# 24 of 48 blocks of modulations move from the first layer's projections to its feed-forward part

## The chip, the core and the metric

The kernel runs on one core of a Trainium2 chip. The metric is the device time of one execution in microseconds (us), the median of several runs; lower is better. The engines are TensorE (PE in the profile; PEld is its weight load), VectorE (DVE), ScalarE (ACT), GpSimd (POOL) and SyncE (SP, whose queue issues nearly all loads here).

## The reference

A block of two layers is followed by two more ("hybrid") layers. Each of the four layers scales and shifts its input by modulations, which are a vector times a wide matrix, and which depend on nothing that the layers compute. Cut to what matters:

```
def adaln(cond, w, b):
    return jax.nn.silu(cond) @ w + b            # w: 1024 x 6144

def modulate(x, g, shift, scale):
    return rmsnorm(x, g) * (1 + scale) + shift

def even_layer(x, c, ctx, c_ctx, ...):          # the first layer
    sh_m, sc_m, gt_m, sh_f, sc_f, gt_f = jnp.split(adaln(c, mod_w, mod_b)[:, None, :], 6, axis=-1)
    sh_c, sc_c = jnp.split(adaln(c_ctx, mod_w, mod_b), 6, axis=-1)[:2]
    p = modulate(x, mix_pre_g, sh_m, sc_m) @ w_in
    uc = modulate(ctx, mix_pre_g, sh_c, sc_c)
    h_m = mlstm_mixer(...)                      # 8 heads
    h_d = diff_mixer(...)                       # 4 heads
    mix = jnp.concatenate([h_m, h_d], axis=-1) @ w_out
    x = x + gt_m * rmsnorm(mix, mix_post_g)
    y = swiglu(modulate(x, ffn_pre_g, sh_f, sc_f), ffn_w1, ffn_w3, ffn_w2)
    return x + gt_f * rmsnorm(y, ffn_post_g)

def odd_layer(...):                             # convolution, then 8 experts; modulations from its own mod_w
def hybrid_layer(x, c, w_ada, b_ada, ...):      # twice; shift, scale, gate from c @ w_ada + b_ada (1024 x 3072)
```

There are 256 tokens of width 1024, all in fp32.

## The kernel before

**The stream.** All weights pass through one list, `plan()` (L1933), which class `Stream` works off in order. An entry is two halves of up to 512 KB. `load_to` issues the two loads on SP's queue (L164) into a ring of RB = 8 buffers named `raw`; a load waits until the buffer eight loads back is free. Most entries are weight chunks: a half is split into a rounded part `hi` (ACT, L98) and the rest `lo` (DVE, L99; both are 128x1024), and then its `raw` buffer is free. The split parts lie in a ring of SB = 5 buffers until PE has used them, each product as three matmuls (L92 to L94). The order in the list is therefore the order of the loads.

**The modulations.** An entry can also be a block of a modulation: 128 rows of one third of a modulation matrix (class `Ada`; a third is a group of 8 blocks, and `it((l, i))` names group i of layer l). Its two halves are multiplied by that row's entry of the condition and added up in the tile `adac`: DVE does the first half (L339 for a group's first block, else L342), ACT scales the second half (L343; L340 for the first block) and POOL adds it in two pieces (L345). After the eighth block PE sums over the rows in 8 matmuls (L359) and transposes (L369), and DVE adds the bias (L372). The blocks of the hybrid layers' last groups, (2,1) and (3,1), have half the width, 512 KB for the whole block. Only group (0,0), which comes first, goes another way (L359 directly).

**The first layer.** `s[0]` is the input projection, 14 chunks in the order of `ORDER` (L486); `Mix0.project` takes one after another and puts the heads between them (table `AFTER`): `diff_unit` for a head of the differential attention, `mlstm_head` for the others. After the first chunk of keys the gates are made: a running maximum over time in 16 steps on DVE (L602), which ends in L612. Chunks with a rotary embedding go through `rope` on DVE (L668, L673, L675), which frees the PSUM bank for the next products. `s[1]` is the output projection, 4 chunks.

**The feed-forward part.** `swiglu_specs` gives 33 chunks: eleven steps of w1, w3 and the w2 of the step before, 1 MiB each. The products of w1 and w3 go to `ph`, those of w2 to `py`.

`weave(a, b, first)` (L1905) spreads list b evenly between the entries of a from entry `first` on. The tile framework then orders each engine's instructions by a timeline of its own when the program is built; on an engine they run in that order. The experts of the second layer get ten more `raw` buffers (RX).

Of the kernel before, what the change touches and what calls it, by code (L numbers as in the profile page):

```python
# [113 lines left out]
class Stream:  # L114
# [8 lines left out]
    def __init__(self, env, plan, ahead, split_ahead=1):  # L123
        self.env, self.plan = env, plan
        self.nd = self.ns = self.n = 0
        self.ahead, self.split_ahead = ahead, split_ahead
        self.raw, self.spl = {}, {}

        self.gain = {}

        self.every = self.turn2 = 0
        self.on_pool = set()
        self.pool, self.bufs, self.more, self.turn = env.rawp, env.raw_bufs, None, 0

        self.stop, self.hold = 1 << 30, (0, [])
# [85 lines left out]
def kchunk(w, n=256):  # L221

    return (4, n, [[(w[512 * n * h:512 * n * (h + 1)].rearrange("(p k f) -> p k f", p=128, k=4), 0, n)] for h in range(2)]), None
# [16 lines left out]
def rchunk(w, r0):  # L240

    return (1, 1024, [[(w[r0 + 128 * h:r0 + 128 * h + 128, :].rearrange("(a p) f -> p a f", p=128), 0, 1024)]
                      for h in range(2)]), None
# [252 lines left out]
def mix0_specs(w_in, w_out):  # L496
    return [kchunk(w_in[i]) for i in range(len(ORDER))], [rchunk(w_out, 256 * i) for i in (2, 3, 0, 1)]
# [445 lines left out]
def swiglu_specs(w1, w3, w2):  # L943
    s = []
    n = w1.shape[0]
    for i in range(n):
        s += [kchunk(w1[i]), kchunk(w3[i])]
        if i:
            s.append(rchunk(w2, 256 * (i - 1)))
    return s + [rchunk(w2, 256 * (n - 1))]  # L950
# [43 lines left out]
def conv_specs(pw1, pw2):  # L994
    s = []
    for i in range(4):
        s += [kchunk(pw1[4 * j + i]) for j in range(2)]
    return s + [rchunk(pw2, 256 * i) for i in range(4)]
# [129 lines left out]
def moe_specs(w1, w3, w2):  # L1128
    s = []
    for x in range(NE):  # L1130
        for i in range(STEPS):
            s += [kchunk(w1[x, i]), kchunk(w3[x, i])]
            if i:
                s.append(rchunk(w2[x], 256 * (i - 1)))
        s.append(rchunk(w2[x], 256 * (STEPS - 1)))
    return s
# [241 lines left out]
def hyb_specs(w_in, w_out, cmp_w1):  # L1378
    s, at = [], 0
    for c in CH:  # L1380
        n = sum(m for _, m in c)
        s.append(kchunk(w_in[D * at:D * (at + n)], n))
        at += n
    s.insert(8, ((1, 1024, [[(cmp_w1[i][:, None, :], 0, 1024)] for i in range(2)]), "raw"))
    return s + [rchunk(w_out, 256 * i) for i in OUT]
# [507 lines left out]

RB, SB, AH, SA, RX, MA, F1, NF = 8, 5, 5, 1, 10, 9, 2, 45


def load_tok(e, ap, t, q=None):
# [5 lines left out]
def weave(a, b, first=0):  # L1905

    out, j, n = list(a[:first]), 0, max(1, len(a) - first)
    for i, x in enumerate(a[first:]):
        k = len(b) * (i + 1) // n
        out += [x, *b[j:k]]  # L1910
        j = k
    return out + list(b[j:])


class Model:
# [17 lines left out]
    def plan(self):  # L1933
        self.moe_start = self.moe_end = 0
        I, it = self.I, self.items
        p = []
        if "l0_mod_w" in I:
            p += it((0, 0))
            s = mix0_specs(I["l0_w_in"], I["l0_w_out"])
            f = it((0, 1), (0, 2), (1, 0), (1, 1), (1, 2), (2, 0))  # L1940
            p += [s[0][0], ((1, D, [[(I["ctx"][0, 128 * b:128 * b + 128, :].rearrange("(a p) f -> p a f", p=128), 0, D)]
                                    for b in range(2)]), lambda *t: self.context(*t))]
            p += weave(s[0][1:], f[:NF], F1) + weave(s[1], f[NF:])
            self.ffn_start = len(p)
            p += weave(swiglu_specs(I["l0_ffn_w1"], I["l0_ffn_w3"], I["l0_ffn_w2"]), it((2, 1), (3, 0), (3, 1)))
        elif "l1_mod_w" in I:
            p += it((1, 0), (1, 1), (1, 2), (2, 0), (2, 1), (3, 0), (3, 1))
        else:
            p += it((2, 0), (2, 1), (3, 0), (3, 1))
        if "l1_mod_w" in I:  # L1950
            p += conv_specs(I["l1_conv_pw1_w"], I["l1_conv_pw2_w"])
            self.moe_start = len(p)
            p += moe_specs(I["l1_moe_w1"], I["l1_moe_w3"], I["l1_moe_w2"])
            self.moe_end = len(p)
        if "w_ada_2" in I:
            for l in range(2):
                p += hyb_specs(I["w_in_2"][l], I["w_out_2"][l], I["cmp_w1_2"][l])
        return p
# [372 lines left out]
```

## Time and profile before

| | |
|---|---|
| median of 3 runs | 1983.44 us (1973.08 to 2013.95) |
| the profiled execution | 1975.42 us, its span 1973.7 us |
| busy share of the span | PE 92%, PEld 82%, DVE 78%, ACT 60%, POOL 23% |
| SP's queue | 464.38 MB, 237 GB/s on the mean over the span |

The first layer's projections and heads run to about 345 us, the feed-forward part from 358 to 562 us, the convolution and the experts of the second layer to about 1540 us, the hybrid layers to the end. A window's row gives, after its stretch and length, busy time and count for PE, PEld, DVE, ACT and POOL, then the share of TensorE's clock that was granted (1.00 is 2.4 GHz, 0.50 is 1.2 GHz), the busy share of the DMA engines and GB/s. A row of the waits gives who waited for whom, the us in all, how often, and the longest. The timeline gives start and length in us.

### The profile page before, as it was taken

How to read it: one execution, taken by the hardware profiler on the slowest of the kernel's cores; microseconds unless marked ns; L12 is line 12 of the kernel's file. 1: busy time of each engine (PE TensorE's matmuls, PEld its weight loads, DVE VectorE, ACT ScalarE, POOL GpSimd, SP SyncE). 2: the span in 40 equal slices, each digit the busy share in tenths (PEclk: the TensorE clock that was granted, in tenths of full speed). 3: DMA queues.
4: the chain of work that ended last, by engine and by line, in shares of the span. 5: the costliest groups of instructions: out<-in, count | busy, mean ns of one | idle time of the engine just before them, and what ended most of it. 6: DMA issues, size and time to landing. Idle time of an engine off the chain costs nothing. (4 is left out here: it accounts for less than half of the span.)

```text
span 1973.7 us, 34412 instructions
## 1 busy us (share of the span) xinstructions
PE 1822.5 (92%) x13059; PEld 1616.2 (82%) x13059; DVE 1531.9 (78%) x2250; ACT 1179.1 (60%) x1804; POOL 454.0 (23%) x351
## 2 busy tenths in 40 slices
PE   6789989799979879999999999999999699989997
PEld 3678677699867568999999999999999589878886
DVE  5887898767664268999999999999998486659675
ACT  4455465655443346777777777777777454454443
POOL 1645664514211141000000000000000442533151
PEclk9889899899989989999999999999999799989999
DMA  9856666588763128999999999999996342344220
GB/s 360 280 182 214 213 227 238 179 269 302 244 247 119 39 80 296 367 348 333 351 363 347 337 351 363 350 330 353 364 352 241 110 142 74 100 128 132 76 76 22
DMA packets 132466, 468.49 MB, mean 237 GB/s; under 512 B 14994, under 2 KB 16274, under 8 KB 132292
## 3 DMA queue, kind: packets, MB, share of 16 engines
q1 hardware_dynamic: 131008, 464.38, 67.0%
q8 instruction: 105, 1.72, 0.4%
q10 hardware_dynamic: 1172, 1.66, 0.2%
q14 instruction: 69, 0.57, 0.1%
q0 software_dynamic: 112, 0.17, 0.1%
HBM read 465.10 MB, written 1.05 MB: 236 GB/s over the span
## 5 line engine op out<-in xcount | busy, mean ns | idle before, releaser
L99 DVE TENSOR_TENSOR lo<-raw,hi 128x1024 fp32r<-128x1024 f32 x694 | 871.7, 1271 | 170.8 <-ACT hi L98 146.1
L98 ACT CAST hi<-raw 128x1024 fp32r<-128x1024 f32 x734 | 762.9, 1048 | 280.4 <-PE ph L94 98.2
L94 PE MATMUL ph<-hi,gl 128*128 128x256 f32 x1408 | 397.7, 283 | 4.4 <-DVE gl L99 4.4
L93 PE MATMUL ph<-lo,gh 128*128 128x256 f32 x1408 | 397.0, 282 | 1.4 <-DVE lo L99 1.0
L92 PE MATMUL ph<-hi,gh 128*128 128x256 f32 x1408 | 394.6, 280 | 0.0
L93 PEld LDWEIGHTS ph<-lo,gh 128*128 128x128 f32 x1408 | 265.4, 188 | 9.9 <-DVE lo L99 5.8
L94 PEld LDWEIGHTS ph<-hi,gl 128*128 128x128 f32 x1408 | 265.4, 189 | 8.0 <-DVE gl L99 4.6
L92 PEld LDWEIGHTS ph<-hi,gh 128*128 128x128 f32 x1408 | 265.6, 189 | 2.8
L345 POOL TENSOR_TENSOR adac<-adac,raw 128x512 f32<-128x512 f32 x112 | 196.5, 1778 | 177.9 <-ACT raw L343 103.9
L1609 POOL MEMSET kv<- 64x2 f32 x4 | 0.4, 96 | 786.3 <-DVE lo L99 776.8
L93 PE MATMUL pe<-lo,hhi 128*128 128x512 f32 x352 | 137.8, 392 | 0.0
L92 PE MATMUL pe<-hi,hhi 128*128 128x512 f32 x352 | 136.9, 396 | 0.5 <-ACT hhi L98 0.5
L99 POOL TENSOR_TENSOR lo<-raw,hi 128x1024 fp32r<-128x1024 f32 (+1 forms) x40 | 97.0, 2433 | 146.1 <-ACT hi L98 120.0
L94 PE MATMUL pe<-hi,hlo 128*128 128x512 f32 x352 | 125.8, 392 | 0.0
L92 PE MATMUL ht<-hi,Hh 128*128 128x256 f32 (+1 forms) x384 | 115.2, 300 | 0.6 <-ACT u L461 0.6
L93 PE MATMUL ht<-lo,Hh 128*128 128x256 f32 (+1 forms) x384 | 114.3, 298 | 0.0
L94 PE MATMUL ht<-hi,Hl 128*128 128x256 f32 (+1 forms) x384 | 113.6, 296 | 0.0
L92 PE MATMUL ph<-Fh,hi 128*128 128x256 f32 x352 | 100.3, 287 | 8.0 <-DVE h L982 6.3
L93 PE MATMUL ph<-Fl,hi 128*128 128x256 f32 x352 | 100.0, 285 | 0.2 <-DVE Fl L475 0.2
L94 PE MATMUL ph<-Fh,lo 128*128 128x256 f32 x352 | 99.4, 285 | 0.0
L92 PEld LDWEIGHTS ht<-hi,Hh 128*128 128x128 f32 x384 | 77.5, 202 | 3.2 <-issue 1.4
L93 PEld LDWEIGHTS ht<-lo,Hh 128*128 128x128 f32 x384 | 77.2, 201 | 1.7 <-issue 1.5
(604 smaller groups left out, 3979.5 us busy)
## 6 DMA issues: line engine op xcount, KB each, us to landing
raw<-in_l_moe_w SPq DMA_DIRECT2D x528, 512.0 KB, 5.3
raw<-in_l_mod_w SPq DMA_DIRECT2D x96, 512.0 KB, 5.6
raw<-in_l_ffn_w SPq DMA_DIRECT2D x66, 512.0 KB, 4.6
raw<-in_w_in SPq DMA_DIRECT2D x60, 512.0 KB, 3.6
raw<-in_w_ada SPq DMA_DIRECT2D x32, 512.0 KB, 5.1
raw<-in_l_w_in SPq DMA_DIRECT2D x28, 512.0 KB, 6.1
raw<-in_l_conv_pw_w SPq DMA_DIRECT2D x24, 512.0 KB, 4.6
raw<-in_w_ada SPq DMA_DIRECT2D x32, 256.0 KB, 4.1
```

What stands on the lines that cost most here:

```text
L92: mm(out, a[0], b[0], start=start, stop=False, **kw)
L93: mm(out, a[0], b[1], start=False, stop=False, **kw)
L94: return mm(out, a[1], b[0], start=False, stop=stop, **kw)
L98: nc.scalar.copy(hi, src)
L99: (lo_eng or nc.vector).tensor_tensor(lo, src, f32(hi), op=OP.subtract)
L345: nc.gpsimd.tensor_tensor(a[:, 1, i:i + 512], a[:, 1, i:i + 512], y[:, i:i + 512], op=OP.add)
L1609: nc.gpsimd.memset(kv[64:128, :, T - 1:T], 0.0)
```

## The change

In the list, three groups of 8 blocks, (1,1), (1,2) and (2,0), move from the first layer to the feed-forward part, which now holds 48 blocks between its 33 chunks, in place of 24. The three groups left, (0,1), (0,2) and (1,0), are spread behind the projection's sixth chunk after the first one (F1 = 5, before 2), three blocks to a chunk; before it were four, and the last three of (2,0) stood between the chunks of the output projection. Nothing else is changed; the same bytes are loaded and the same sums made.

```
-RB, SB, AH, SA, RX, MA, F1, NF = 8, 5, 5, 1, 10, 9, 2, 45
+RB, SB, AH, SA, RX, MA, F1 = 8, 5, 5, 1, 10, 9, 5
...
-            f = it((0, 1), (0, 2), (1, 0), (1, 1), (1, 2), (2, 0))
+            f = it((0, 1), (0, 2), (1, 0))
...
-            p += weave(s[0][1:], f[:NF], F1) + weave(s[1], f[NF:])
+            p += weave(s[0][1:], f, F1) + s[1]
...
-            p += weave(swiglu_specs(I["l0_ffn_w1"], I["l0_ffn_w3"], I["l0_ffn_w2"]), it((2, 1), (3, 0), (3, 1)))
+            p += weave(swiglu_specs(I["l0_ffn_w1"], I["l0_ffn_w3"], I["l0_ffn_w2"]), it((1, 1), (1, 2), (2, 0), (2, 1), (3, 0), (3, 1)))
```

What stands on DVE ahead of the first `rope` (its first row is L668; `adac` is a modulation's sum, `lo` a weight chunk's rest, `u`, `Ul`, `qT` and `nlam` belong to the layer). Before:

```order
L342 SCALAR_TENSOR_TENSOR adac<-raw,cond_112,adac 128x1024
L99 TENSOR_TENSOR lo<-raw,hi 128x1024
L445 TENSOR_SCALAR u<-kT,g_464,modc 128x256 x2
L650 SCALAR_TENSOR_TENSOR qT<-cvt,cvy 128x256
L824 TENSOR_SCALAR nlam<-nlam 128x1
L446 TENSOR_TENSOR Ul<-u,Uh 128x2x256
L650 SCALAR_TENSOR_TENSOR qT<-cvt,cvy 128x256
L342 SCALAR_TENSOR_TENSOR adac<-raw,cond_112,adac 128x1024
L575 MEMSET lf 128x4x24
L99 TENSOR_TENSOR lo<-raw,hi 128x1024
L668 TENSOR_TENSOR rp_551<-pk,rope_291 128x256
L342 SCALAR_TENSOR_TENSOR adac<-raw,cond_112,adac 128x1024
```

The same place now:

```order
L824 TENSOR_SCALAR nlam<-nlam 128x1
L650 SCALAR_TENSOR_TENSOR qT<-cvt,cvy 128x256
L445 TENSOR_SCALAR u<-kT,g_464,modc 128x256
L99 TENSOR_TENSOR lo<-raw,hi 128x1024
L446 TENSOR_TENSOR Ul<-u,Uh 128x2x256
L650 SCALAR_TENSOR_TENSOR qT<-cvt,cvy 128x256
L575 MEMSET lf 128x4x24
L339 TENSOR_SCALAR adac<-raw,cond_112 128x1024
L99 TENSOR_TENSOR lo<-raw,hi 128x1024
L668 TENSOR_TENSOR rp_551<-pk,rope_291 128x256
```

Of the five sums of the first group that stood ahead of this rope's end or between its rows (L339 once, L342 four times), one is left, the L339 that opens the group.

SP's queue where the feed-forward part begins (`in_l_ffn_w` its chunks, two loads each; `in_w_ada` and `in_l_mod_w` blocks of modulations). Before:

```order
L164 DMA raw<-in_l_w_out 128x1024 x2
L164 DMA raw<-in_w_ada 128x1024 x2
L164 DMA raw<-in_l_ffn_w 128x1024 x4
L164 DMA raw<-in_w_ada 128x512 x2
L164 DMA raw<-in_l_ffn_w 128x1024 x2
L164 DMA raw<-in_w_ada 128x512 x2
L164 DMA raw<-in_l_ffn_w 128x1024 x4
L164 DMA raw<-in_w_ada 128x512 x2
```

Now:

```order
L164 DMA raw<-in_l_w_out 128x1024 x8
L164 DMA raw<-in_l_ffn_w 128x1024 x2
L164 DMA raw<-in_l_mod_w 128x1024 x2
L164 DMA raw<-in_l_ffn_w 128x1024 x2
L164 DMA raw<-in_l_mod_w 128x1024 x2
L164 DMA raw<-in_l_ffn_w 128x1024 x2
L164 DMA raw<-in_l_mod_w 128x1024 x4
L164 DMA raw<-in_l_ffn_w 128x1024 x2
```

One or two blocks of full width now stand between any two chunks, where one or none of half the width stood.

## Rows read from the trace of the kernel before

**Rows 1.** Windows in the first layer: stretch, length, engines, PEclk, DMA share, GB/s.

```profile
20.00:40.00 20.00, 13.99 (x74) 8.10 (x75) 11.17 (x20) 12.17 (x19) 4.28 (x5) 0.91 1.02 403
60.00:80.00 20.00, 6.98 (x36) 6.56 (x37) 19.96 (x22) 5.34 (x6) 13.42 (x8) 0.66 0.73 241
100.00:120.00 20.00, 20.00 (x120) 17.05 (x119) 19.52 (x25) 10.39 (x13) 18.25 (x12) 1.00 0.76 258
120.00:140.00 20.00, 14.09 (x78) 10.97 (x76) 15.56 (x28) 9.29 (x19) 3.16 (x6) 0.74 0.43 138
220.00:240.00 20.00, 15.40 (x56) 10.70 (x58) 19.93 (x25) 8.74 (x15) 16.80 (x15) 0.86 0.84 283
240.00:260.00 20.00, 15.76 (x88) 9.86 (x84) 18.75 (x27) 10.48 (x19) 11.50 (x7) 0.84 0.79 269
300.00:320.00 20.00, 16.94 (x107) 14.41 (x107) 19.90 (x28) 14.20 (x25) 16.23 (x10) 0.91 0.95 342
```

**Rows 2.** Waits of PE in 40:85, 118:142, 218:262: us, times, longest.

```profile
PE pf L92 <- DVE rp L673: 13.9, 1, 13.9
...
PE ds L833 <- DVE mscan L612: 4.0, 1, 4.0
...
PE ds L841 <- DVE de L839: 5.3, 2, 4.6
```

**Rows 3.** Timeline of DVE, 50:80: start and length in us, then the work.

```profile
52.67 2.31 DVE L342 SCALAR_TENSOR_TENSOR adac<-raw,cond,adac 128x1024 f32<-128x1024 f32 x1
54.90 0.68 DVE L446 TENSOR_TENSOR Ul<-u,Uh 128x512 fp32r<-128x512 f32 x1
...
59.74 2.28 DVE L342 SCALAR_TENSOR_TENSOR adac<-raw,cond,adac 128x1024 f32<-128x1024 f32 x1
...
64.13 1.68 DVE L446 TENSOR_TENSOR Ul<-u,Uh 128x512 fp32r<-128x512 f32 x1
...
66.06 1.27 DVE L342 SCALAR_TENSOR_TENSOR adac<-raw,cond,adac 128x1024 f32<-128x1024 f32 x1
...
67.37 2.17 DVE L99 TENSOR_TENSOR lo<-raw,hi 128x1024 fp32r<-128x1024 f32 x1
...
69.80 1.95 DVE L342 SCALAR_TENSOR_TENSOR adac<-raw,cond,adac 128x1024 f32<-128x1024 f32 x1
```

**Rows 4.** Timeline of DVE, 100:142: two steps of the running maximum.

```profile
108.87 1.41 DVE L602 TENSOR_TENSOR mscan<-mscan 32x256 f32<-32x256 f32 x1
...
125.59 0.41 DVE L602 TENSOR_TENSOR mscan<-mscan 32x256 f32<-32x256 f32 x1
```

**Rows 5.** Windows: feed-forward part to its middle, within it, and the experts.

```profile
358.00:466.00 108.00, 104.62 (x729) 95.82 (x730) 76.17 (x75) 60.13 (x78) 42.74 (x39) 0.98 0.80 266
440.00:480.00 40.00, 40.00 (x278) 37.44 (x278) 33.09 (x27) 23.99 (x29) 20.53 (x12) 1.00 0.94 336
760.00:800.00 40.00, 40.00 (x286) 37.49 (x285) 37.59 (x39) 32.13 (x39) 0.00 (x0) 1.00 1.00 371
```

**Rows 6.** Tiles ph, py (358:466), py: ns min/median/max, first and last start.

```profile
L92 PE MATMUL ph<-Fh,hi x352: 277/283/416, 358.5 to 549.8; 128*128 128x256 f32 x176
...
L94 PE MATMUL py<-hi,hlo x40: 388/389/389, 390.9 to 464.6; 128*128 128x512 f32 x40
...
L94 PE MATMUL py<-hi,hlo x88: 388/389/486, 390.9 to 561.6; 128*128 128x512 f32 x88
```

**Rows 7.** Timeline of the SP queue, 335:375.

```profile
341.43 4.06 SPq L164 DMA_DIRECT2D raw<-in_w_ada  x2
362.46 6.87 SPq L164 DMA_DIRECT2D raw<-in_l_ffn_w  x4
```

**Rows 8.** The page, one group: busy us, mean ns, idle before.

```profile
L99 DVE TENSOR_TENSOR lo<-raw,hi 128x1024 fp32r<-128x1024 f32 x694 | 871.7, 1271 | 170.8 <-ACT hi L98 146.1
```

**Rows 9.** Timeline of PE, 493:495: the closing sum of one group.

```profile
493.38 1.06 PE L359 MATMUL adap<-adac,ones 128*32 128x512 f32 x8
```

## The prediction

> **What bounds the kernel now.** I read the windows first, since the share of busy time over the whole span mixes parts with different limits. In the first layer [rows 1] PE is the engine that should never rest, but after the start (20 to 40, where the first loads set the pace) it is idle for 3 to 13 us of 20 in five of six windows, and DVE is busy there for 18.8 to 20 us, or has just been so (from 100 to 120). The granted clock falls to 0.66 to 0.91 in the same windows, so PE also runs part of the time at 1.2 GHz after it rested. The waits [rows 2] name DVE each time: 13.9 us for the first rope, 4.0 us for the end of the running maximum (L612), 5.3 us for the mixing of the two softmax maps. So in this part DVE ends last, and POOL makes it worse: the same step of the running maximum takes 0.41 us alone and 1.41 us in the stretch where POOL adds blocks for 18.25 of 20 us [rows 1, 4]. DMA is not short there: four of the six load 138 to 269 GB/s, one 283.
>
> The feed-forward part is the opposite [rows 5]: from 358 to 466 us PE is busy for 104.6 of 108 us, DVE for 76 of them, and 266 GB/s are loaded. It is bound by PE, with slack in DVE and in DMA. Where the full-width blocks stood, 440 to 480 us, the slack was thin: DMA share 0.94 at 336 GB/s, DVE 33.1 of 40 us. In the experts, with more buffers and pure weight chunks, 371 GB/s is a DMA share of 1.00: that is where loading ends.
>
> So the change takes work away from the part where DVE is late and puts it where PE hides everything, until DMA no longer keeps up. One gain and one loss decide, and I size them apart. The profiled execution took 1975.4 us, near the lowest of the runs; the median, 1983.4, lies 8 above it.
>
> **What the first layer gets back.** Five places.
>
> (a) The first rope. DVE is busy without a break here, and before the rope's end stand one L339 and four L342 of 2.31, 2.28, 1.27 and 1.95 us [rows 3], 7.8 us together. The order shows that the four go and an L339 stays. The neighbours also lose what POOL's adds cost them: 1.68 us for the L446 that took 0.68 before, 2.17 us for an L99 that takes 1.27 on the mean [rows 3, 8], so 1.9 us in two rows. That is 9.7 us at least; the wait itself, 13.9 us [rows 2], and the lower clock behind it bound it at some 16. I take 12, nearer to what I can count.
>
> (b) The running maximum. PE idles 5.9 us from 120 to 140 and loses up to 5 more to the clock (0.74) [rows 1], so 11 at most. The order has three sums of blocks and four L99 between the first step and the last, and two and two now, and POOL adds fewer blocks beside it. The blocks that remain still come here, so it could also gain nothing. I take 4.
>
> (c) 220 to 260. PE idles 4.6 and 4.2 us and loses up to 6 to the clock [rows 1], 15 at most. DVE is busy for 38.7 of 40 us. Counted in the order from the fourth mLSTM head to the sixth, 17 sums of blocks become 12; five at 1.3 to 2.3 us [rows 3] are 6 to 11 us of DVE. PE waits only for a part of DVE's work, so 6.
>
> (d) 300 to 320. 3.1 us idle and up to 1.8 of the clock [rows 1]. No sum of a block stands behind the fifth head now. I take 4 of the 4.9.
>
> (e) Three closing sums on PE (L359), 1.06 us each [rows 9], leave a part that PE bounds for one where they can hide in its waits for loads: 3 us.
>
> Together 29 us. The bounds add up to 10 from below (only (a) is counted in rows) and to 50 from above, but all five at their upper end would mean that nothing else is late next; heads and units still wait for each other's results, so I use 45.
>
> What is new in a queue: the loads of chunks 4 to 6 now go out ahead of the first block, so those chunks land earlier. The L339 in front of the rope waits for its block, which is loaded behind these six halves. If it lands late, the rope waits in DVE's queue behind it. That is inside the lower end of (a).
>
> **What the feed-forward part pays.** PE's work there is the same, so it can't be shorter. The first 24 blocks are of 1.049 MB each and stand between the first 17 chunks of the same size (48 blocks to 33 chunks). When its first product starts, at 358.5 us [rows 6], the ring has been full since 341 and 4 us more pass until SP issues again [rows 7]. In the ring now lie block, chunk, block, chunk, and one chunk is split ahead. So 22 blocks and 14 chunks are still to come, 37.7 MB. At rate r the last lands 4 us + 37.7/r after the start. Then come the rounding, the subtraction (1.27 us [rows 8]) and the products of one chunk, some 8 us in all, an estimate from the 6.06 us a chunk below. PE took 106.5 us for these 17 chunks: from 358.5 to the end of the fortieth triple of `py`, 464.6 + 0.4 [rows 6]. The 16 chunks after them took 97.0 us, to 562.0, or 6.06 us each.
>
> For r I have 336 GB/s, where PE was still the slower, so DMA could have done more with eight buffers, and 371, its limit with eighteen [rows 5]. I take the middle, 353. Then 4 + 106.8 + 8 = 118.8, 12.3 us more than PE needed. In the next 5.5 chunks, with 8 blocks of half the width (10.0 MB, 28.2 us, against 33.3 of PE), the ring gets 5.1 us ahead. In the 5.5 chunks with (3,0) (14.2 MB, 40.1 us) it falls 6.8 behind, so 1.7 remain. The last stretch is like the second and costs nothing. That is 14 us.
>
> DVE and POOL have to keep up as well. From 440 to 480 they were busy 33.1 and 20.5 us of 40 [rows 5], or 5.0 and 3.1 us per chunk at 0.73 blocks a chunk. With 1.45, DVE's L342 at 1.27 to 2.31 us makes 5.9 to 6.7 and POOL 6.2, against 7.2 us of DMA per chunk (2.53 MB). So DMA still ends last, but closely, and an L342 that waits for its block holds up the product of SwiGLU (L982) behind it on DVE, for which PE waits. I add 4 us (0 to 8). That makes 18; at 371 GB/s it is 7 and at 336, with the 4, 27. Ahead of the part, one chunk less is split while the residual is computed, since a block stands second in the list; its split lies behind the 5.6 us or more of the first chunk's products, so I cost it at nothing, and at 2 us if PE waits for it.
>
> **Rivals.** *The loss wins.* The ring of eight turns over more slowly, because each half of a block waits for DVE, or for ACT and then POOL, in their queues. The price of 29 us is reached at 332 GB/s by the sum above, just under the 336 that was seen; below that the kernel is slower. In the window from 220 to 240, where POOL was busy for 16.8 of 20 us, the ring delivered 283 GB/s [rows 1], and PE still waited for DVE. At that rate the first stretch costs 38.7 us, the others 18.9, with the 4 some 62: 1975.4 - 29 + 62 = 2008. Against it speaks that SP's ring ran at 336 with chunks and blocks mixed.
>
> *The gain is small.* Behind the first rope, another wait takes the place of each that is shortened: the blocks still come with three to a chunk, and DVE's own work of the heads remains. Then (a) and (e) are left, 15 us, and with the loss of 18 it is 1978.
>
> *No loss.* From 20 to 40 us the same eight buffers took in 403 GB/s [rows 1], with a consumer that freed them at once. At that rate the first stretch needs 4 + 93.5 + 8 = 105.5 us, less than PE, and nothing is lost: 1975.4 - 29 = 1946. Against it speak 371 GB/s at a DMA share of 1.00 in the experts. The Trainium skill (DMA: Bandwidth & Descriptors, section Measured (HBM→SBUF, 128 partitions, SWDGE, issued from GpSimd)) has 425 GB/s for a core that streams alone and about 358 where its neighbour streams too; by the first figure this rival would hold. The experts' row is nearer to the second, so I give it little.
>
> That the change doesn't do what it says is excluded by the order: 47 sums of blocks stood on DVE between start and residual, now 24, and 48 in place of 25 behind it.
>
> **How the numbers follow.** Forecast: 1975.4 - 29 + 18 = 1964, chance 0.55. The gain is small: 1978, 0.2. The loss wins: 2008, 0.15. No loss: 1946, 0.1. The forecast's own bounds are -45 + 7 and -10 + 27, 1937 to 1992. For 8 in 10 I leave out the better part of the lowest corner and the upper half of the rival that ends slower, and allow for a median that lies some us above a good run: 1942 to 1999. About 2% is what a measurement of this kernel can tell from no change. From the median of before that is 1944 and 2023: faster 0.07, slower 0.04, within 0.89.
>
> **What would show it.** The wait for the first rope in 40 to 85 should fall from 13.9 us to under 4, and the first product of the feed-forward part should start at about 330 us, not 358. The feed-forward part should take about 221 us, not 203.5, and its first 17 chunks about 120, with DMA share over 0.95 at 340 to 365 GB/s, and PE waiting there for splits. (b) to (d) are wrong if DVE is as full from 100 to 320 us as before. The loss is wrongly sized if the DMA share stays under 0.9 while PE waits (then DVE, POOL or the ring sets the pace), or if PE doesn't wait at all. The whole is wrong if the experts or later parts change by more than some us, since nothing of theirs moves.

## The result, and the profile after

The changed kernel took 2007.52 us (median of four runs, 2000.99 to 2010.04) against 1983.76 for the one before, a ratio of 1.0108 with a 95% interval of 1.0067 to 1.0149: about 1% slower, and outside the range of 1942 to 1999. Ratios compare fast runs alone: a run over 1.5% above the fastest of its kernel is left out of the ratio, though not of the medians. The profiled execution has a span of 2004.9 us against 1973.7.

The profile splits that difference. Stages are told apart by events that both traces have: the first product of the feed-forward part, its last product, the first modulated input of each hybrid layer, and the last product of the last one.

| us | before | after | difference | forecast |
|---|---|---|---|---|
| start to the feed-forward part | 358.5 | 331.9 | -26.6 | -29 |
| feed-forward part | 203.5 | 236.6 | +33.1 | +18 |
| residual behind it, convolution, experts, the way into the hybrid layers, the end behind the last product | 995.7 | 1001.0 | +5.3 | 0 |
| first hybrid layer | 207.5 | 219.3 | +11.8 | 0 |
| second hybrid layer | 208.5 | 216.1 | +7.6 | 0 |
| span | 1973.7 | 2004.9 | +31.2 | -11 |

The first event in the changed kernel, in place of the first of [rows 6]: the first product starts at 331.9 us, about 330 was forecast.

```profile
L92 PE MATMUL ph<-Fh,hi x352: 274/283/580, 331.9 to 557.1; 128*128 128x256 f32 x176
```

The gain came as forecast. The loss beside it was nearly twice as large, and a further loss stands where nothing was moved. Of the third row, the experts are equal (798.2 and 798.0).

**First layer.** The windows that answer to [rows 1], in the changed kernel:

```profile
60.00:80.00 20.00, 17.59 (x124) 15.46 (x123) 9.34 (x11) 7.67 (x12) 6.15 (x8) 1.00 0.60 193
...
120.00:140.00 20.00, 20.00 (x147) 18.09 (x148) 10.55 (x22) 11.50 (x26) 0.27 (x4) 0.94 0.21 65
...
240.00:260.00 20.00, 14.54 (x94) 12.67 (x93) 20.00 (x21) 11.44 (x23) 15.28 (x10) 0.81 0.73 241
300.00:320.00 20.00, 19.50 (x91) 15.45 (x89) 11.23 (x21) 8.11 (x15) 1.88 (x2) 1.00 0.41 133
```

From 60 to 80 us PE is busy for 17.6 us, not 7.0, and DVE for 9.3, not 20. The same stretch of time now holds later work, but the picture is the same at 120 and at 300: DVE no longer fills the window. At 240 it still does, for the blocks that stayed.

What PE waits for, in 30:85, 85:142 and 218:262, a row of each, in place of [rows 2]:

```profile
PE pf L92 <- ACT Uh L444: 2.3, 1, 2.3
...
PE ds L833 <- DVE mscan L612: 0.5, 1, 0.5
...
PE ds L841 <- DVE de L839: 9.1, 2, 5.5
```

The wait of 13.9 us for the rope is gone, that for the running maximum fell from 4.0 to 0.5, that for the mixing of the two maps rose from 5.3 to 9.1.

**Feed-forward part.** The whole part before, then the whole part and three windows of it in the changed kernel:

```profile
358.00:562.00 204.00, 197.03 (x1364) 180.04 (x1364) 138.90 (x141) 107.51 (x142) 63.14 (x51) 0.99 0.79 265
...
332.00:568.00 236.00, 211.53 (x1377) 188.43 (x1378) 205.91 (x164) 132.20 (x160) 145.06 (x89) 0.94 0.89 314
...
340.00:360.00 20.00, 11.64 (x77) 11.43 (x76) 19.94 (x12) 10.69 (x13) 19.18 (x13) 0.74 0.90 312
400.00:420.00 20.00, 16.36 (x82) 12.35 (x83) 19.95 (x14) 8.72 (x11) 15.70 (x8) 0.91 0.94 337
...
500.00:520.00 20.00, 20.00 (x137) 18.43 (x135) 19.55 (x16) 12.33 (x14) 15.91 (x8) 1.00 0.99 373
```

PE is idle for 24.5 us in place of 7.0 and busy for 211.5 in place of 197.0, at a mean granted clock of 0.94, not 0.99: the loss is somewhat more than half waiting, and the rest is PE's own work at the lower clock. In the first two of the three windows, where PE waits, DVE is busy for 19.9 of 20 us and POOL for 16 to 19, while DMA has a share of 0.90 to 0.94 and delivers less than the 373 GB/s of the third window. So DVE ends last there, not the loads. The waits of PE in the part say the same:

```profile
PE ph L94 <- DVE lo L99: 11.2, 5, 2.9
PE ph L92 <- DVE h L982: 8.4, 1, 8.4
PE py L92 <- ACT hi L98: 2.4, 1, 2.4
```

The timeline from 396 to 412, DVE's rows and the one of POOL beside them:

```profile
394.64 13.40 POOL L345 TENSOR_TENSOR adac<-adac,raw 128x512 f32<-128x512 f32 x6
...
395.68 4.55 DVE L342 SCALAR_TENSOR_TENSOR adac<-raw,cond,adac 128x1024 f32<-128x1024 f32 x2
...
400.16 4.50 DVE L99 TENSOR_TENSOR lo<-raw,hi 128x1024 fp32r<-128x1024 f32 x2
404.58 2.30 DVE L342 SCALAR_TENSOR_TENSOR adac<-raw,cond,adac 128x1024 f32<-128x1024 f32 x1
...
410.18 1.27 DVE L342 SCALAR_TENSOR_TENSOR adac<-raw,cond,adac 128x1024 f32<-128x1024 f32 x1
```

As long as POOL adds (2.23 us for each of six), an L342 takes 2.28 us and a split L99 2.25. Two us after POOL has ended, L342 is back at 1.27. DVE is full less of new work than of instructions that take longer; how much of each the experiments tell.

**Hybrid layers.** The build orders an engine's instructions by its own timeline, and here it came out otherwise, though no line of these layers was touched. PE's order in the middle of the first hybrid layer, where four transpositions at a time (L386) broadcast gates that ACT then copies (L387). Before:

```
L1715 MATMUL as<-HTh,HTl 128x128 x2
L386 MATMUL bg<-ident,mod_1_674 128x128 x4
L1497 MATMUL hx<-ident,hr 128x128 x4
L1715 MATMUL as<-HTh,HTl 128x128 x2
L1715 MATMUL as<-HTh,hnrl 128x128 x2
L1715 MATMUL as<-HTh,HTl 128x256 x4
L1715 MATMUL as<-HTh,hnrl 128x256 x2
L386 MATMUL bg<-ident,mod_1_674 128x128 x4
```

After:

```
L94 MATMUL hf<-Hh,lo 128x256
L386 MATMUL bg<-ident,mod_1_674 128x128 x8
L1497 MATMUL hx<-ident,hr 128x128 x4
L92 MATMUL hf<-Hh,hi 128x256
```

The eight now stand together. PE's timeline shows the price, in the kernel before:

```profile
1614.71 0.63 PE L1497 MATMUL hx<-ident,hr 128*128 128x128 f32 x4 [0.71 <-DVE hnrl L99]
...
1618.43 0.62 PE L386 MATMUL bg<-ident,mod 128*128 128x128 f32 x4 [0.79 <-DVE kv L1608]
1620.13 1.09 PE L1497 MATMUL hx<-ident,hr 128*128 128x128 f32 x4 [1.08 <-DVE HTh L99]
...
1622.52 1.11 PE L386 MATMUL bg<-ident,mod 128*128 128x128 f32 x4
```

and in the changed one:

```profile
1629.59 0.62 PE L386 MATMUL bg<-ident,mod 128*128 128x128 f32 x4 [1.95 <-DVE kv L1608]
1632.60 1.11 PE L386 MATMUL bg<-ident,mod 128*128 128x128 f32 x4 [2.38 <-ACT hgtb L387]
1634.23 1.08 PE L1497 MATMUL hx<-ident,hr 128*128 128x128 f32 x4 [0.52 <-DVE hnrl L99]
```

The second four wait 2.38 us for ACT to copy the first four, where other products stood between them; the three waits make 4.9 us in place of 2.6. Some 25 us later the clock falls as well, in a window in which PE is busy throughout:

```profile
1658.00:1678.00 20.00, 20.00 (x116) 17.14 (x116) 10.30 (x48) 9.06 (x32) 0.93 (x2) 0.74 0.10 28
```

0.74 of 2.4 GHz over 20 us is 10.4 us at 1.2 GHz. The kernel before had the full clock at the same distance from the layer's start, but a lower one in the window ahead, again with a busy PE:

```profile
1626.20:1646.20 20.00, 20.00 (x153) 16.94 (x152) 14.26 (x63) 8.22 (x29) 0.90 (x2) 0.83 0.23 75
1646.20:1666.20 20.00, 20.00 (x166) 18.75 (x163) 11.95 (x52) 11.00 (x33) 3.71 (x4) 1.00 0.23 65
```

So the whole first hybrid layer has to be compared, not one window: by its mean clock (0.936 before, 0.897 after) some 27 us of it ran at 1.2 GHz before and some 45 after. The order of the second hybrid layer differs in some 20 rows of PE and 6 of DVE, ACT's in none.

### The profile page after: what moved, and what is told of

It reads as the page before. It is cut to its first block, busy times and chain, and to the rows that moved or that the text cites. A ratio compares the mean times of both kernels' runs of the same rounds, so it can differ in the third digit from the quotient of the medians.

```text
span 2004.9 us, 34408 instructions
## 1 busy us (share of the span) xinstructions
PE 1847.0 (92%) x13059; PEld 1638.8 (82%) x13059; DVE 1540.7 (77%) x2250; ACT 1180.8 (59%) x1804; POOL 459.3 (23%) x351
## 3 DMA queue, kind: packets, MB, share of 16 engines
q10 hardware_dynamic: 1172, 1.66, 0.2%
HBM read 465.10 MB, written 1.05 MB: 233 GB/s over the span
## 5 line engine op out<-in xcount | busy, mean ns | idle before, releaser
L99 DVE TENSOR_TENSOR lo<-raw,hi 128x1024 fp32r<-128x1024 f32 x694 | 887.0, 1294 | 148.5 <-ACT hi L98 121.9
L98 ACT CAST hi<-raw 128x1024 fp32r<-128x1024 f32 x734 | 762.3, 1048 | 262.5 <-PE ph L94 97.9
L345 POOL TENSOR_TENSOR adac<-adac,raw 128x512 f32<-128x512 f32 x112 | 203.3, 1839 | 138.1 <-ACT raw L343 96.2
L99 POOL TENSOR_TENSOR lo<-raw,hi 128x1024 fp32r<-128x1024 f32 (+1 forms) x40 | 95.5, 2395 | 138.5 <-ACT hi L98 120.8
L92 PE MATMUL ht<-hi,Hh 128*128 128x256 f32 (+1 forms) x384 | 115.9, 302 | 0.6 <-ACT u L461 0.6
L92 PEld LDWEIGHTS ph<-Fh,hi 128*128 128x128 f32 x352 | 71.0, 202 | 15.1 <-DVE h L982 8.6
L94 PEld LDWEIGHTS ph<-Fh,lo 128*128 128x128 f32 x352 | 69.2, 203 | 14.7 <-DVE lo L99 13.0
```

What stands on the lines that cost most here:

```text
L92: mm(out, a[0], b[0], start=start, stop=False, **kw)
L94: return mm(out, a[1], b[0], start=False, stop=stop, **kw)
L98: nc.scalar.copy(hi, src)
L99: (lo_eng or nc.vector).tensor_tensor(lo, src, f32(hi), op=OP.subtract)
L345: nc.gpsimd.tensor_tensor(a[:, 1, i:i + 512], a[:, 1, i:i + 512], y[:, i:i + 512], op=OP.add)
```

## The experiments

Two questions: is the loss behind the experts one of the order (theory 1), of the moved loads, or of the clock alone? And is the loss in the feed-forward part one of DVE and POOL slowing each other (theory 2), of the loads, or of DVE's own work? All stages, us, each from one profiled execution ("the rest" is the third row of the table above); ratios with 95% intervals against runs of the kernel before on the same chip.

| kernel | start | feed-forward | the rest | hybrid 1 | hybrid 2 | span | median | ratio |
|---|---|---|---|---|---|---|---|---|
| before, again | 366.0 | 202.8 | 1000.6 | 210.3 | 208.8 | 1988.5 | 1988.9 | 0.999 [0.995, 1.004] |
| after, again | 331.0 | 234.0 | 1003.1 | **222.7** | 213.2 | 2004.0 | 2009.6 | 1.010 [1.006, 1.014] |
| before, F1 = 5 | 389.4 | 199.6 | 999.5 | 207.7 | 211.9 | 2008.1 | 2010.3 | 1.010 [1.004, 1.017] |
| after, F1 = 3 | 328.9 | 237.3 | 997.9 | 202.3 | 208.7 | 1975.1 | 1989.8 | 0.998 [0.993, 1.004] |
| the move, F1 = 2 | 332.6 | 234.9 | 1002.9 | 206.5 | 208.9 | 1985.8 | 1997.9 | 1.012 [1.005, 1.020] |
| 40 blocks in the part | 338.9 | 214.0 | 998.6 | 210.2 | 210.5 | 1972.2 | 1975.3 | 0.996 [0.991, 1.000] |
| after, no POOL adds | 330.4 | 207.6 | 1005.9 | **217.0** | 226.2 | 1987.1 | one run | - |
| after, loads only | 329.7 | 205.3 | 1000.7 | 207.6 | 211.8 | 1955.1 | one run | - |
| sums on DVE, 48, F1 = 3 | 329.2 | 216.9 | 997.2 | 210.4 | 210.5 | 1964.2 | 1972.9 | 0.992 [0.989, 0.995] |
| sums on DVE, 40, F1 = 6 | 340.8 | 206.0 | 1000.5 | 210.2 | 217.9 | 1975.4 | 1976.8 | 0.997 [0.993, 1.002] |
| the same, F1 = 4 | 329.9 | 204.5 | 1000.3 | **219.3** | 216.4 | 1970.4 | one run | - |
| all sums on DVE, 48, F1 = 5 | 317.4 | 218.1 | 1002.0 | 210.8 | 217.9 | 1966.2 | one run | - |
| before, NF = 44 | 365.9 | 205.2 | 997.7 | **220.7** | 208.7 | 1998.2 | 2001.6 | 1.008 [1.004, 1.011] |
| before, NF = 46 | 360.5 | 203.2 | 996.0 | 210.4 | 217.7 | 1987.8 | one run | - |
| all sums on DVE, 40, F1 = 5 | 330.4 | 205.2 | 1001.7 | 205.2 | 215.5 | 1958.0 | 1959.5 | 0.984 [0.979, 0.989] |

In bold: kernels whose build orders the first hybrid layer on DVE and ACT as, or nearly as, in the changed one. All others have the order of before there; on PE it differs by a few rows among them.

**Both kernels once more.** No edit.

Before: 

> The kernel before once more, with nothing changed. Between the two profiles the changed kernel gained 26.7 us until the feed-forward part begins (358.5 to 331.8), lost 33.2 in it (203.5 to 236.7) and some 5 in the convolution, and lost 19.4 in the two hybrid layers, from their first modulated input to the last product of the output (416.0 to 435.4). Theory 1: the loss in the hybrid layers belongs to the changed kernel, because the build ordered their instructions differently. Then this run shows 416 us there, within 3. Theory 2: it is the granted clock of the one execution that was profiled (half speed for 60 us in these layers before, for 96 after). Then this run can show anything from 412 to 436 us. Both: a ratio of 1.00, 203 us in the feed-forward part.

After: 

> The changed kernel once more, with nothing changed. Theory 1 (order): 435 us in the hybrid layers, within 3. Theory 2 (the clock of one execution): anything from 412 to 436. Both: feed-forward part begins at 332, takes 237 us, ratio 1.011 within its interval.

The loss stands (ratio 1.010), and the hybrid layers take 419.1 and 435.9 us, 3 and 0.5 from the first pair. The kernel before alone moves by 7.5 us up to the feed-forward part (358.5 and 366.0) with the clock (mean 0.954 and 0.942 over the whole). So differences of some us in one profile prove nothing by themselves; 33 and 31 us in the feed-forward part do, and 12 in the first hybrid layer need more kernels.

**Parts of the change.** F1 = 3 in the changed kernel:

```
-RB, SB, AH, SA, RX, MA, F1 = 8, 5, 5, 1, 10, 9, 5
+RB, SB, AH, SA, RX, MA, F1 = 8, 5, 5, 1, 10, 9, 3
```

> The changed kernel with F1 = 3 in place of 5: the 24 blocks come from the projection's fourth chunk after the first on, so somewhat more thinly. The feed-forward part is the changed one, with 48 blocks. But the build orders the hybrid layers' instructions on PE, DVE and ACT exactly as in the kernel before. Theory 1 (order): 416 us in the hybrid layers; with the feed-forward part at 237 us and the first layer between 332 and 345 us, the whole some 8 us slower than before, 1983 on the scale of the profiles. Theory 2 (clock): the order there doesn't matter, 412 to 436 by chance.

F1 = 5 in the kernel before, without the move:

```
-RB, SB, AH, SA, RX, MA, F1, NF = 8, 5, 5, 1, 10, 9, 2, 45
+RB, SB, AH, SA, RX, MA, F1, NF = 8, 5, 5, 1, 10, 9, 5, 45
```

> The kernel before with F1 = 5 alone: the six groups stay in the first layer and come from the sixth chunk on, five or six blocks to a chunk; the feed-forward part keeps its 24 blocks and 203.5 us. The order in the hybrid layers is that of before but for two products. My step (a): the wait for the first rope (13.9 us) goes, since no block stands ahead of it. If that place were all that counts, the feed-forward part begins 12 us earlier, at 346. Rival: DVE's and POOL's work is only put off, and the denser blocks behind give it back: no earlier than 356. Theory 1: 416 us in the hybrid layers.

The move without F1:

```
-RB, SB, AH, SA, RX, MA, F1 = 8, 5, 5, 1, 10, 9, 5
+RB, SB, AH, SA, RX, MA, F1 = 8, 5, 5, 1, 10, 9, 2
```

> The move of the 24 blocks alone: F1 stays 2, as before. DVE and ACT run the hybrid layers in the order of before. Theory 1 (the order of the hybrid layers costs the change 17 to 20 us): hybrid layers 410 to 420 us together, feed-forward part 232 to 239, start of it between 326 and 342, in all 1975 to 1998, within 1% of the kernel before. Rival (it is the moved loads or the clock, whatever the order): hybrid layers 430 us or more, 2000 to 2012 in all. If F1 = 5 was worth something for the first layer, the feed-forward part begins 3 us or more later than the 331 of the changed kernel.

F1 = 3 gives the hybrid layers the order of before and they take 411.0 us, not 435; start and feed-forward part are those of the changed kernel. The same 24 blocks in the same part thus cost nothing there under the other order. F1 = 5 without the move puts the same 45 blocks between fewer chunks and begins the feed-forward part 31 us later than before (23 later than the second profile of before): the rival holds, the denser blocks give the rope's gain back and more. With the move, F1 = 2 or 5 begin it at 332.6 and 331.9: F1 = 5 ends the first rope earlier (59.4 us, not 68.5), but the running maximum ends at 109.0 and 108.3, so nothing of that lasts. The stages of the move alone are as theory 1 has them (415.4 in the hybrid layers), but of its four timed runs the profiled one is the fastest, and the ratio of 1.012 is over the forecast of 1%; no trace shows where the other runs lost it, so this kernel's time stays unexplained.

**What the feed-forward part waits for.** First, no adds on POOL for the late blocks:

```
-            for i in range(0, self.n // 2, 512):
+            for i in range(0, 0 if getattr(self, "late", False) else self.n // 2, 512):
```

> The changed kernel, with POOL's adds (L345) left out for the six groups whose blocks stand in the feed-forward part, so half of each of those sums is missing; loads, DVE's and ACT's work stay. Theory 2, that DVE and POOL slow each other there and so hold the ring and the splits: the feed-forward part falls from 234 to 237 us to 205 to 217, L99 and L342 in it from 2.25 us to under 1.5, PE's idle time from 24 us to under 12. Rival, loading sets the pace (48 blocks and 33 chunks are 83 MB at what DMA gives): it stays above 225, DMA share at 0.9 or more wherever PE waits. Rival, DVE has too much to do even by itself: it stays above 225 with DVE busy for over 19 of 20 us in those windows.

Second, only the loads and each group's first sum:

```
-        if vec:
+        if vec and not (getattr(self, "late", False) and k):
```

> The changed kernel, with all sums of blocks but each group's first (L342, L343, L345) left out for the six groups whose blocks stand in the feed-forward part; the loads stay. It shows what the loading of 48 blocks alone costs. By the prediction's sum for DMA (14 us over 203.5, at 353 GB/s) the part takes 211 to 218 us; if loading costs nothing, 200 to 206; if loading alone explains the loss, 228 to 238. Theory 2 says 203 to 217 and 3 us or less below the kernel without POOL's adds; the rival that DVE's own load decides says that this one is at least 10 us below it.

207.6 and 205.3 us. (The loads that the first text counts are 76.5 MB, not 83: 16 of the 48 blocks have half the width.) The windows from 340 and from 400 without POOL's adds:

```profile
340.00:360.00 20.00, 18.38 (x146) 17.84 (x146) 15.65 (x17) 13.73 (x17) 3.39 (x3) 1.00 1.02 412
400.00:420.00 20.00, 18.76 (x132) 16.97 (x128) 13.84 (x16) 12.95 (x15) 0.00 (x0) 1.00 1.03 418
```

The one from 340 with the loads alone:

```profile
340.00:360.00 20.00, 20.00 (x150) 18.32 (x150) 11.70 (x15) 10.91 (x15) 2.70 (x3) 1.00 1.02 415
```

The splits over the part without POOL's adds:

```profile
L99 DVE TENSOR_TENSOR lo<-raw,hi x66: 1216/1224/1602, 333.7 to 534.4; 128x1024 fp32r<-128x1024 f32 x66
```

Without POOL's adds, but with the same loads, the same sums on DVE and the same scaling on ACT, the ring takes in 412 GB/s where it took 312, DVE is busy for 15.7 us and not 19.9, and no split is longer than 1.60 us (median 1.22; 1.48 and up to 4.62 in the changed kernel). Over the part DVE is busy for 147.9 us, 58.0 less, without having lost one instruction: with 70 adds on POOL that is 0.83 us of DVE for each. So the 33 us are, to the 2 or 3 us by which single profiles differ: loads 1.8 (205.3 - 203.5), sums on DVE and scaling on ACT 2.3, POOL's adds 29.0. Theory 2 holds, both rivals fall. One thing isn't separated: without its adds POOL also no longer holds its half of a block, for which SP's queue waited 43 us in the changed kernel (some 140 for DVE). But in the four stretches where PE idles most there (332 to 352, 392 to 412, 432 to 452, 512 to 532; 3.4 to 8.1 us each), DVE itself is busy for 19.3 to 20.0 us, so it wasn't short of loads.

The Trainium skill (SBUF — State Buffer, section Who interferes with whom) says that a DVE instruction with two inputs in SBUF contends with a GpSimd instruction that reads SBUF. The trace agrees: L99 and L342 (two inputs each) go from 1.22 and 1.27 to 2.25 and 2.28 us, and ACT's L98 keeps its 1.05. The prediction hadn't weighed this rule.

**Fewer blocks moved.** One group goes back to the first layer:

```
-            f = it((0, 1), (0, 2), (1, 0))
+            f = it((0, 1), (0, 2), (1, 0), (1, 1))
...
-            p += weave(swiglu_specs(I["l0_ffn_w1"], I["l0_ffn_w3"], I["l0_ffn_w2"]), it((1, 1), (1, 2), (2, 0), (2, 1), (3, 0), (3, 1)))
+            p += weave(swiglu_specs(I["l0_ffn_w1"], I["l0_ffn_w3"], I["l0_ffn_w2"]), it((1, 2), (2, 0), (2, 1), (3, 0), (3, 1)))
```

> The changed kernel, with one group given back: 32 blocks in the first layer, 40 in the feed-forward part; DVE and ACT run the hybrid layers in the order of before. Theory 1: hybrid layers 410 to 420 us. If the loss in the feed-forward part begins only past what DVE and POOL can carry, the 16 blocks over before cost less than two thirds of the 33 us (10 to 20: part of 214 to 224), and the first layer gives back 15 to 22: in all 1968 to 1990. If the loss grows evenly by block, 22 us, and it is 1980 to 1995. Rival of theory 1: hybrid layers 430 us or more, 1990 to 2010.

Two thirds of the move cost 10.5 us in the feed-forward part and gave 20 to 27 in front of it. The last group costs 22.6 there and gives 7. So the loss isn't even by block: DVE, busy for 188.4 of 214 us with 40 blocks, has little slack left for the last eight. The hybrid layers take 420.7 us, 0.7 over the forecast. The ratio, 0.996 [0.991, 1.000], is hardly to be told from no change.

**The sums without POOL.** If an add on POOL costs DVE 0.83 us, two of them cost 1.66, and DVE does that half itself in 1.27:

```
             nc.vector.scalar_tensor_tensor(a[:, 0], x, c, a[:, 0], op0=OP.mult, op1=OP.add)
+            if getattr(self, "late", False):
+                nc.vector.scalar_tensor_tensor(a[:, 1], y, c, a[:, 1], op0=OP.mult, op1=OP.add)
+                return
             nc.scalar.activation(y, y, AF.Copy, scale=c)
```

48 blocks, F1 = 3: 

> The move with F1 = 3 (hybrid layers in the order of before) and, in the six groups of the feed-forward part, both halves of a block summed up by DVE (L342 twice), without ACT and POOL. By theory 2 a POOL add costs DVE more than the add itself would: DVE gets 28 more sums of 1.27 us and 14 of 0.75 us, 46 us, on the 140 of 200 us that it was busy without POOL's adds, so it still fits: feed-forward part 207 to 218 us in place of 237, in all 1945 to 1962. Rival: DVE is then full (186 of 200 us) and in order, and PE waits for the splits as before: part 225 us or more, 1965 or more.

40 blocks, F1 = 6: 

> 32 blocks in the first layer, 40 in the feed-forward part with both halves on DVE, F1 = 6; PE, DVE and ACT run the hybrid layers in the order of before. Theory 2: feed-forward part 204 to 212 us (214 with POOL's adds), its start at 335 to 342, hybrid layers 410 to 420 us, in all 1950 to 1966. Rival (DVE full): part 214 us or more.

40 blocks, F1 = 4: 

> The same with F1 = 4, which changes nothing in the feed-forward part, but PE, DVE and ACT run the hybrid layers in the order of the changed kernel. Theory 1 forecasts from the order alone: hybrid layers 432 to 444 us, 15 us or more above the kernel with F1 = 6. Rival (it was what the move does to the parts ahead, the clock, or chance): 410 to 422 us, as there.

All groups, 48 blocks, F1 = 5 (the condition is dropped): 

> The changed kernel (F1 = 5) with every block's second half summed up by DVE, in the first layer too, where DVE ends last. If POOL's adds slow DVE by more than the add costs there as well, the feed-forward part begins at 315 to 330 us (331 before that edit); rival, DVE's own work decides: 21 more sums of 1.27 us, 27 us, put it at 335 to 358. Feed-forward part 207 to 218 us by theory 2. PE's order in the hybrid layers is a third one here, DVE's and ACT's is that of before: theory 1 says 410 to 422 us if DVE's and ACT's order decides.

The parts came in as forecast (the last 0.1 us over): 216.9, 206.0, 204.5 and 218.1 us in place of 237 and 214. With 48 blocks and F1 = 3, DVE is busy for 188.2 of 217 us, and PE still waits for a split and for one product of SwiGLU:

```profile
PE ph L92 <- DVE h L985: 4.8, 1, 4.8
PE ph L94 <- DVE lo L99: 4.0, 2, 3.0
```

In the first layer, where DVE ends last, the same edit brings the start from 331.9 to 317.4: DVE has 21 instructions more, yet it is busy for 219.2 us up to there, not 223.1. The totals of the two timed kernels missed: 1972.9 and 1976.8 us, 11 over the upper end each. In the second of them the second hybrid layer is at 217.9; in the kernel with all sums on DVE it is too, which puts the two layers at 428.7, not at 410 to 422. The forecast from the order alone held for the first hybrid layer, 219.3 against 210.2, and for the sum of both, 435.7, but that is only 7.6 above its twin, not 15.

**One block.** The kernel before with NF = 44 (NF = 46 alike):

```
-RB, SB, AH, SA, RX, MA, F1, NF = 8, 5, 5, 1, 10, 9, 2, 45
+RB, SB, AH, SA, RX, MA, F1, NF = 8, 5, 5, 1, 10, 9, 2, 44
```

NF = 44: 

> The kernel before with NF = 44: one block more stands between the chunks of the output projection (four in place of three), nothing else. The build orders the hybrid layers on DVE and ACT nearly as in the changed kernel. If the order costs the time by itself, the first hybrid layer takes 215 to 223 us (202 to 211 in the kernels with the order of before), both together 430 to 444, and the whole is 0.5 to 1.2% slower. If it is the placement of the 24 blocks that costs it, by some road other than the order: 207 and 208 us, and no change of the whole.

NF = 46: 

> The control: NF = 46, one block fewer there, and the order of the hybrid layers is that of before on PE, DVE and ACT. First hybrid layer 202 to 211 us, both together 411 to 428 (the second one has been at 208 to 218, with the granted clock).

One block moved by a few entries in the first layer, 1200 us earlier, and the first hybrid layer takes 220.7 us, the whole kernel 0.8% longer; both layers together are at 429.4, just under the forecast. In the control, NF = 46, the first takes 210.4. With NF = 44, PE's timeline is that of the changed kernel again:

```profile
1629.06 0.62 PE L386 MATMUL bg<-ident,mod 128*128 128x128 f32 x4 [1.95 <-DVE kv L1608]
1632.07 1.11 PE L386 MATMUL bg<-ident,mod 128*128 128x128 f32 x4 [2.39 <-ACT hgtb L387]
```

and so is the window at the same distance from the layer's start:

```profile
1657.30:1677.30 20.00, 20.00 (x115) 17.07 (x115) 10.25 (x48) 9.17 (x32) 0.93 (x2) 0.74 0.10 28
```

In all kernels, the first hybrid layer takes 202.3 to 210.8 us under the order of before (twelve, mean 208.3) and 217.0 to 222.7 under the other (five, mean 219.8): 11.5 us, and the groups don't meet. In this layer PE idles for 14.9 us on the mean of the twelve and for 19.3 on that of the five, and by the granted clock 28.8 and 42.3 us of it run at 1.2 GHz. From 100 to 120 us behind its start, the clock is 1.00 in all twelve and 0.74 to 0.83 in all five. So 4.4 us of the 11.5 are waits, and the clock accounts for up to 6.8, half of the 13.5 us more at 1.2 GHz. The second one takes 208.5 to 217.9 and 208.7 to 226.2: they overlap, so theory 1 is right for the first layer only. What the second layer adds (7.6 us in the first pair, 4.4 in the second) is no more than kernels with the order of before show among themselves.

**Put together.** All sums on DVE, 32 blocks in the first layer, 40 in the feed-forward part, F1 = 5:

> A version put together from the findings: F1 = 5, 32 blocks in the first layer and 40 in the feed-forward part, both halves of every block but a group's first on DVE; hybrid layers in the order of before. From the stages measured so far: start of the feed-forward part at 318 to 335 us, the part itself 204 to 210, hybrid layers 411 to 428, in all 1938 to 1962, faster than before by 1 to 2.5%. Rival: with one group more in the first layer DVE is the bound there again, start at 340 or more, and it is within 1% of before.

1959.5 us (six runs, 1948.1 to 1986.4), ratio 0.984 [0.979, 0.989]: 1.6% faster than before and the fastest of these kernels. All stages lie in their forecasts. The same kernel with POOL's adds, 40 blocks in the part, has a ratio of 0.996.

## Why the prediction was wrong

**The first layer** was right in sum: 26.6 us in the first pair of profiles, 35.0 in the second (366.0 to 331.0), 29 forecast. Its parts were less so, and it is partly luck that their errors cancel. The rope ends 12.5 us earlier (71.9 to 59.4), (a) had 12. The lead at the first mixing of maps (L841) is 21.7 us, so the running maximum gave 9, (b) had 4. At the last L841 it is 23.7, so (c) gave 2, not 6: the wait for L839 grew in place of others, as "the gain is small" had it for every wait. (d) and (e) together gave 3, not 7. And what F1 = 5 adds at the rope, 9 of the 12.5 us, is gone by 109 us: without it the running maximum ends no later.

**The feed-forward part** is the mis-sized term: 18 forecast, 33.1 measured (31.2 in the second pair). Both of its summands were wrong, in opposite directions. The DMA sum at 353 GB/s said 14; loading costs 1.8, because the ring takes in 412 GB/s when it is freed at once. That was the mechanism of "no loss", with 403 GB/s from [rows 1]; the experts' 371, which was held against it, wasn't the limit here, and why they stay there no run tells. And "I add 4 us (0 to 8)" for DVE stood for 31. The step that failed is "So DMA still ends last, but closely". It compares means, DVE's 5.9 to 6.7 and POOL's 6.2 us per chunk with DMA's 7.2, and as means they were nearly right: over the first 17 chunks DVE was busy for 115.9 us, 6.8 per chunk, and POOL for 94.0, 5.5. But what slows L342 beside POOL slows L99 too: 2.17 us stood in [rows 3], and the prediction used it for the first layer alone. While POOL adds without a break, two L99 of 2.25 and 1.45 L342 of 2.28 are 7.8 us per chunk, and with the rest of DVE's work (SwiGLU's product, its split) more than the 7.2 of DMA and the 6.06 of PE. So there are stretches of 20 us in which DVE is full, PE waits and its clock falls, and others in which PE is busy throughout and DVE's slack is of no use (372 to 392 us: PE 20.0, DVE 12.5). The first 17 chunks took 132.7 us, not 119, the last 16 took 104.0, not 97. The sign named for this case, a DMA share under 0.9 while PE waits, came true in part: in the windows from 340, 400, 440 and 520 us the share is 0.90, 0.94, 0.83 and 0.84. That DVE sets the pace is seen from its own busy time and from the run without POOL's adds.

**"The loss wins"** gave 2008, and the kernel took 2007.5, but not by its mechanism: it had the ring slowed to 283 GB/s and 62 us lost there, with nothing lost elsewhere. That the two numbers meet is luck.

**The hybrid layers** are the step that failed outright: "nothing of theirs moves". The order was read where the change acts, and the rest was taken as given, though the order of every later part was there to be compared. It would have shown hundreds of moved rows on PE, with the eight transpositions together; it would not have given their price. The runs put that at 11.5 us in the first hybrid layer, 4.4 of it in waits of PE (2.3 at that place in the first pair), the rest with more time at 1.2 GHz. What in the new order makes the clock fall 25 us later isn't settled, nor are 3 us more in the residual behind the feed-forward part (16.5 to 19.5 us in both pairs). These go with the 48 blocks: 17.6 to 20.7 us in the eight kernels that have them, 16.5 to 16.8 in the nine others.

With 33 for the loss, 11.5 for the order and 29 for the gain the change costs 15.5 us. That is within what was measured: 1.0067 to 1.0149 of 1983.8 us is 13 to 30 us longer.

## What to carry to other kernels

Before work is moved under an engine with slack, take off that slack what the engines beside it cost each other: an add on POOL cost DVE 0.83 us here, so half of a sum was cheaper on the busy DVE itself (1.27 us) than on the idle POOL (1.66), and with 40 blocks in the part moving it brought the ratio from 0.996 to 0.984, where moving the blocks alone lost 1%. Where a program orders its instructions when it is built, compare the order of every part with that of before, also of those that the edit doesn't touch, and try neighbours of a tuning number: one block's place decided 0.8%. Compare busy times by stretches too, not as means alone: DVE's mean fitted here, and PE waited all the same. A time that is right by two errors is no test of the reasons; stages are.

## What the runs showed that I had not expected

- DVE and POOL slow each other nearly twofold when both run on: L99 1.22 to 2.25 us, L342 1.27 to 2.28, POOL's add of 128x512 1.27 to 2.23. ACT's L98 keeps its 1.05.
- With eight buffers of 512 KB freed at once, one queue took in 410 to 418 GB/s at a DMA share of 1.02 to 1.03, beside a PE that was busy for 18.4 to 20 of 20 us; the experts, at 371 and a share of 1.00, had looked like the limit.
- The same program differs by 7.5 us up to the feed-forward part in two profiled executions, and by up to 9 in the second hybrid layer between kernels with nearly the same order there (208.5 us at a mean granted clock of 0.944, 217.9 at 0.883).
